# A decoder layer on one core: gate and projection products dealt out anew between the steps of two attention branches

## Chip, cores and metric

The kernel runs on one core of a Trainium2 chip. The metric is device time in microseconds (us) of one execution; lower is better. All tensors are fp32. The large products run in a split form: an fp32 matrix is taken apart into a rounded high part and the rest, and a product of two such pairs is made of three matmuls.

## The reference, cut to what matters

```python
h = rms_norm(x, g_mix)                       # x: 512 tokens x 1024
z = h @ w_in                                 # -> qa, ka, va, qb, kb, vb, gate logits gl
ya = swa_sink_attention(rms(qa), rms(ka), va, sinks, bias_a)   # window 128, 8 q heads, 2 kv heads
# differential branch, per head (4) and block of 128 queries:
p = softmax(where(causal, q @ k.T / 8 + bias_b, -inf))         # two maps, c = 0, 1
ob = (p[0] - lam * p[1]) @ vb
yb = rms_norm(ob, subln_b) * (1 - lam_init)
g = sigmoid(gl)                              # two gates of 1024
x = x + (g[0] * (ya @ w_br_a) + g[1] * (yb @ w_br_b)) @ w_o
u = causal_dwconv3(rms_norm(x, g_ffn) @ w_up)
x = x + (silu(u_gate) * u_value) @ w_down
```

## The kernel before, in words

All weights lie in one array of units of 128 x 1024. `wunit(u)` (L132) loads a unit over SP's queue, rounds it on ACT (L123, tile whi) and subtracts on POOL or DVE (L124, tile wlo); each call also starts the unit behind it in the fixed order `worder` (AHEAD = 1). So a unit's split is issued when the unit ahead of it begins, which is eight steps earlier for most units. `mm3` (L143) makes one **step** of three matmuls: L145 and L147 need whi, and one of L146 and L147 needs wlo.

The program has three stretches. First the query, key and value products of the window branch. Then, from about 52 to 305 us, both attention branches. Last the output product, the MLP and the down product, which are matmuls without a break.

In the middle stretch each unit of attention is a chain: PE scores, DVE adds the bias and takes the maximum, ACT takes the exponentials, DVE normalises, PE transposes, ACT and DVE round the transposed weights, PE multiplies with the values. PE would wait for each of these, so independent products are dealt between its steps: gates, the two differential projections DA and DB, the differential values VB and the window branch's output product. They stand in one queue, a `Stream`, in a fixed order. `fill(name, i)` takes so many steps from the queue's head as the table FILL says, and `until(name)` takes all that are left of one kind. PE, and PE alone, runs in the order in which the code is written (`manual_schedule`); the orders of DVE, ACT and POOL are made by the scheduler at build time, and each engine keeps its own order when it runs.

The window branch has eight units (four query blocks times two kv heads), here called window unit 0 to 7. Its queue holds three gates (24 steps), DA (32) and five gates (40): 96 steps. The loop is

```python
    for i in range(nu + 2):
        if i < nu:
            swa_score(*swa[i])
        fill("s1", i)
        if 0 <= i - 1 < nu:
            swa_trans(*swa[i - 1])
        fill("s2", i)
        if 0 <= i - 2:
            swa_av(*swa[i - 2])
        fill("s3", i)
```

Ahead of it stand `fill("q")`, the query transposes, `fill("k")`, the key transposes (L415) and `fill("k2")`. Behind it stand `fill("p0")`, `diff_parts` for head 0 (transposes L415, rounding in L424, L426, L436, L438, L439), `fill("p1")`, the same for head 1, and `until("ga")`, which takes what is left of the 96. Then the eight sigmoids of the first gates are issued (L486, on ACT), VB, the output product, DB and eight gates are put into the queue (160 steps), and `fill("p2")` follows.

The differential branch has sixteen units, four heads times four blocks, here differential unit 0 to 15. For unit i the code scores it (L443, L444; a[i] steps behind), then transposes unit i - 1 (L705; b[i - 1] steps behind). The product with the values of a head (L725, `diff_av`) comes once a head, heads 2 and 3 get their `diff_parts` ahead of units 8 and 9 (f steps behind), and DB is finished ahead of unit 6. Lines that the text names: L572 bias and maximum, L588 normalise, L597 transpose, L601 rest of the rounding, L614 and L616 the product with the values (window); L678, L683, L689, L705, L712, L725 the same steps (differential).

Of the kernel before, what the change touches and what calls it, by code (L numbers as in the profile page):

```python
# [59 lines left out]

FILL = dict(v=[9, 17, 25, 33], m=[0, 0, 0, 0], r=[4, 9, 13, 18], o=[7, 11, 15, 17], e=[1, 1, 0, 40], kv=4,
            up=3, warm=8, q=3, k=19, k2=4, s1=[0, 3, 2, 2, 2, 3, 3, 0, 0, 3],
            s2=[3, 1, 0, 3, 1, 3, 5, 2, 0, 1], s3=[3, 0, 4, 1, 3, 2, 1, 6, 0, 1], p0=4, p1=7, p2=6, ud=6,
            pd=[8, 9], f=[7, 0], a=[7, 1, 4, 6, 12, 3, 0, 3, 0, 1, 7, 2, 4, 0, 0, 7],
            b=[6, 2, 4, 4, 2, 7, 2, 1, 2, 0, 2, 2, 1, 0, 3, 2], c=[6, 0, 0, 2], d=[1, 1, 0, 5])
AHEAD = 1
EARLY = 5

# [2 lines left out]
def tile_decoder_layer(ctx: ExitStack, tc: tile.TileContext, x4, wall, cst_d, relb_d, oneh_d, xn_d, out):  # L73
# [35 lines left out]
    def at():  # L109
        return psum.tile([P, S], F32, tag="ps", name=nm("at"))  # L110
# [72 lines left out]
    def along_free(col, alloc, between=None):  # L183

        ch = stat.tile([P, NT], F32R, tag="colh", name=nm("colh"))
        cl = stat.tile([P, NT], F32, tag="coll", name=nm("coll"))
        nc.vector.tensor_copy(ch, col)
        nc.vector.tensor_tensor(cl, col, ch.bitcast(F32), ALU.subtract)
        ps = at()
        for i, part in enumerate((ch.bitcast(F32), cl)):  # L190
            dg = alloc().bitcast(F32R)
            for t in range(NT):
                nc.vector.tensor_scalar(dg[:, t * P:(t + 1) * P], ident, part[:, t:t + 1], None, ALU.mult)
            nc.tensor.matmul(ps, ones, dg, start=i == 0, stop=i == 1)
            if between is not None and i == 0:
                between()
        return ps
# [18 lines left out]
    ps = at()  # L216
    for i in range(FILL["warm"]):
        nc.tensor.matmul(ps, zero[:, :P], zero, start=True, stop=True)
# [269 lines left out]
    class Stream:  # L488
# [18 lines left out]
        def fill(self, n):  # L507
            while n > 0 and self.step():
                n -= 1
# [7 lines left out]
    def fill(name, i=None):  # L517
        fs.fill(FILL[name] if i is None else FILL[name][i])

# [123 lines left out]
    def diff_parts(z, hh):  # L643
        qs = q_parts(pair_T(z, hh * 256), gqa[:, 1:2])
        kh, kl = k_parts(pair_T(z, hh * 256 + P), cst[:, C_KNB:C_KNB + 1])
        return qs, kh, kl
# [90 lines left out]
    def diff_out(h):  # L737
        o, col = dpo.pop(h)
        r = along_free(col, otile, lambda: fs.fill(FILL["m"][h]))
        nc.vector.tensor_tensor(o, o, r, ALU.mult)  # L740
# [38 lines left out]
    def products(place):  # L779
        for h in range(4):  # L780
            if FILL["v"][h] == place:
                fs.until("vb")
# [4 lines left out]
    for i in range(len(todo) + 1):  # L787
        if i < len(todo):
            h, b = todo[i]
            if i == FILL["ud"]:  # L790
                fs.until("db")
            for h1 in (2, 3):
                if i == FILL["pd"][h1 - 2]:
                    qkt[h1] = diff_parts(zt[2], h1 - 2)
# [265 lines left out]
```

## Time and profile before

| | |
|---|---|
| median of 3 runs | 734.42 us (734.22 to 736.84) |
| profiled execution | 734.53 us |
| its span on the core | 732.7 us |
| mean granted TensorE clock | 0.988 |
| PE, DVE, ACT, POOL busy | 97%, 63%, 43%, 23% of the span |

The profiled execution is one run of the program with the hardware profiler; its own time is the span plus what lies around it (1.8 us). The three runs are timed without it.

### The profile page before, as it was taken

What the parts mean: (1) busy time and instruction counts of PE and PEld (TensorE: products, weight loads), DVE (VectorE), ACT (ScalarE), POOL (GpSimd) and SP (SyncE); (2) the same over time, 40 slices, a digit from 0 to 9 for tenths busy, and PEclk for the clock granted to TensorE, in tenths of its full rate; (3) what the DMA queues carried; (4) which work ended last, traced back from release to release, by engine and by line L of the source; (5) the groups of instructions that cost most, each with busy time, mean ns of one, the idle gap of its engine ahead of it and who ended that gap; (6) DMA issues with size and microseconds to landing.
All of it is one profiled execution on the core that took longest, in us unless ns stands there. A gap on an engine that the chain in (4) does not pass through costs nothing.

```text
span 732.7 us, 8962 instructions
## 1 busy us (share of the span) xinstructions
PE 708.0 (97%) x3312; PEld 585.0 (80%) x3312; DVE 458.3 (63%) x940; ACT 315.3 (43%) x522; POOL 167.5 (23%) x130
## 2 busy tenths in 40 slices
PE   8999996999999889989999999999999999999998
PEld 5887785878887768868888888888888888888888
DVE  5688799576409798595438876766666674322220
ACT  6554674754336436444325444444444442221220
POOL 1154235454435320083400201110110110000000
PEclk9999998999999999999999999999999999999999
DMA  8762111132132020225421332322322322333310
GB/s 310 278 219 87 58 58 46 42 114 82 63 105 69 30 81 35 86 78 167 155 89 59 115 114 87 104 97 87 109 92 88 115 80 85 132 114 102 114 65 30
DMA packets 21820, 74.04 MB, mean 101 GB/s; under 512 B 2612, under 2 KB 3152, under 8 KB 21648
## 3 DMA queue, kind: packets, MB, share of 16 engines
q1 hardware_dynamic: 18976, 65.02, 26.2%
q0 software_dynamic: 1360, 6.34, 2.7%
q10 hardware_dynamic: 1440, 2.11, 0.8%
q8 instruction: 26, 0.43, 0.2%
q14 instruction: 18, 0.15, 0.1%
HBM read 71.34 MB, written 4.47 MB: 103 GB/s over the span
## 4 chain that ended last, share of the span: by engine, by line
PE 83%; DVE 12%; ACT 3%; issue 1%; DMA 1%; SPq 0%; ACTq 0%; DVEq 0%
PE pj L145 26%; PE pj L146 25%; PE pj L147 25%; ACT s L581 1%; PE at L725 1%; DVE s L588 1%; DVE g L850 1%; DVE qv L439 1%; DVE s L572 1%; DVE qv L438 1%; DVE g L849 1%; DMA g<-in_x_dram 1%; PE at L415 1%; PE at L705 1%; PE pj L321 1%
## 5 line engine op out<-in xcount | busy, mean ns | idle before, releaser
L123 ACT ACTIVATE whi<-raw 128x1024 fp32r<-128x1024 f32 (+1 forms) x117 | 121.7, 1044 | 178.3 <-PE pj L146 121.1
L145 PE MATMUL pj<-xg,whi 128*128 128x512 f32 x480 | 190.6, 397 | 0.0
L147 PE MATMUL pj<-xg,wlo 128*128 128x512 f32 x480 | 188.1, 392 | 0.0
L146 PE MATMUL pj<-xg,whi 128*128 128x512 f32 x480 | 187.9, 392 | 0.0
L124 DVE TENSOR_TENSOR wlo<-raw,whi 128x1024 fp32r<-128x1024 f32 (+1 forms) x84 | 103.4, 1234 | 81.9 <-ACT whi L123 81.8
L147 PEld LDWEIGHTS pj<-xg,wlo 128*128 128x128 f32 x480 | 90.7, 189 | 19.1
L145 PEld LDWEIGHTS pj<-xg,whi 128*128 128x128 f32 x480 | 90.8, 189 | 17.9
L146 PEld LDWEIGHTS pj<-xg,whi 128*128 128x128 f32 x480 | 90.8, 189 | 17.7
L124 POOL TENSOR_TENSOR wlo<-raw,whi 128x1024 fp32r<-128x1024 f32 x33 | 79.6, 2417 | 107.6 <-ACT whi L123 88.3
L916 DVE TENSOR_TENSOR u<-pj,rbc 128x512 f32<-128x512 f32 x44 | 30.2, 690 | 48.3 <-PE pj L147 48.3
L145 PE MATMUL pj<-whi,xg 128*128 128x512 f32 (+1 forms) x156 | 58.3, 373 | 0.0
L146 PE MATMUL pj<-wlo,xg 128*128 128x512 f32 (+1 forms) x156 | 57.6, 369 | 0.1
L147 PE MATMUL pj<-whi,xg 128*128 128x512 f32 (+1 forms) x156 | 57.4, 368 | 0.0
L919 ACT ACTIVATE yc<-u,cst 128x512 f32<-128x512 f32 x44 | 35.4, 810 | 4.5 <-DVE u L916 4.5
L145 PE MATMUL pj<-y,whi 128*128 128x512 f32 (+1 forms) x95 | 37.1, 391 | 0.0
L147 PE MATMUL pj<-y,wlo 128*128 128x512 f32 (+1 forms) x95 | 36.4, 383 | 0.2 <-POOL wlo L124 0.2
L147 PE MATMUL pj<-qv,wlo 128*128 128x512 f32 (+1 forms) x94 | 35.4, 377 | 1.1 <-DVE wlo L124 1.1
L146 PE MATMUL pj<-y,whi 128*128 128x512 f32 (+1 forms) x95 | 36.2, 381 | 0.0
L921 DVE SCALAR_TENSOR_TENSOR yc<-u,cst,yc 128x510 f32<-128x510 f32 x44 | 34.8, 794 | 1.3
L145 PE MATMUL pj<-qv,whi 128*128 128x512 f32 (+1 forms) x94 | 35.4, 376 | 0.0
L920 DVE SCALAR_TENSOR_TENSOR yc<-u,cst,yc 128x511 f32<-128x511 f32 x44 | 33.7, 768 | 0.0
L146 PE MATMUL pj<-qv,whi 128*128 128x512 f32 (+1 forms) x85 | 32.3, 380 | 1.5 <-POOL qv L853 1.5
(213 smaller groups left out, 1159.2 us busy)
## 6 DMA issues: line engine op xcount, KB each, us to landing
raw<-in_w_dram SPq DMA_DIRECT2D x109, 512.0 KB, 3.3
raw<-in_w_dram SPq DMA_DIRECT2D x8, 384.0 KB, 3.2
scr<-scr POOLq DMA_DIRECT2D x1, 2304.0 KB, 11.7
xnat<-in_xn_dram SPq DMA_DIRECT2D x2, 1024.0 KB, 9.4
tmp<-in_x_dram POOLq DMA_DIRECT2D x8, 256.0 KB, 3.2
g<-in_x_dram SPq DMA_DIRECT2D x7, 256.0 KB, 7.0
out_dram<-x ACTq DMA_DIRECT2D x7, 256.0 KB, 2.0
bias_a<-scr POOLq DMA_DIRECT2D x1, 1024.0 KB, 7.3
```

Source lines behind the costliest of these rows:

```text
L123: nc.scalar.activation(hi[:, :width], raw[:, :width], AF.Copy)
L124: eng.tensor_tensor(lo[:, :width], raw[:, :width], hi[:, :width].bitcast(F32), ALU.subtract)
L145: nc.tensor.matmul(ps, a[0], b[0], start=start, stop=False)
L146: nc.tensor.matmul(ps, a[0], b[1], start=False, stop=False)
L147: nc.tensor.matmul(ps, a[1], b[0], start=False, stop=stop)
L321: nc.tensor.matmul(banks[t][:, :width], xg[k][a][:, t * P:(t + 1) * P], wk[b], start=(a, b) == (0, 0), stop=False)
L415: nc.tensor.transpose(ps[:, t * P:(t + 1) * P], zs[t][:, c0:c0 + P], ident)
L438: nc.vector.tensor_copy(k[o, :], k[s, :].bitcast(F32))
L916: nc.vector.tensor_tensor(u, ps, rbc2, ALU.mult)
L919: nc.scalar.activation(y, u, AF.Identity, bias=cst[:, C_CB + ch:C_CB + ch + 1], scale=cw[2])
L920: nc.vector.scalar_tensor_tensor(y[:, 1:S], u[:, 0:S - 1], cw[1], y[:, 1:S], ALU.mult, ALU.add)
L921: nc.vector.scalar_tensor_tensor(y[:, 2:S], u[:, 0:S - 2], cw[0], y[:, 2:S], ALU.mult, ALU.add)
```

## The change

Only the table FILL changes. No product is added or removed, and each queue keeps its order; what changes is how many steps of the queue lie at each place.

```diff
-            up=3, warm=8, q=3, k=19, k2=4, s1=[0, 3, 2, 2, 2, 3, 3, 0, 0, 3],
-            s2=[3, 1, 0, 3, 1, 3, 5, 2, 0, 1], s3=[3, 0, 4, 1, 3, 2, 1, 6, 0, 1], p0=4, p1=7, p2=6, ud=6,
-            pd=[8, 9], f=[7, 0], a=[7, 1, 4, 6, 12, 3, 0, 3, 0, 1, 7, 2, 4, 0, 0, 7],
-            b=[6, 2, 4, 4, 2, 7, 2, 1, 2, 0, 2, 2, 1, 0, 3, 2], c=[6, 0, 0, 2], d=[1, 1, 0, 5])
+            warm=8, q=7, k=19, k2=4, s1=[0, 3, 2, 2, 2, 3, 3, 0, 0, 3], s2=[4, 3, 0, 3, 1, 7, 5, 2, 0, 1],
+            s3=[3, 0, 1, 5, 6, 2, 2, 6, 0, 1], p0=4, p1=5, p2=8, ud=6, pd=[8, 9], f=[9, 0],
+            a=[5, 1, 8, 7, 10, 2, 0, 3, 0, 1, 7, 4, 6, 0, 0, 5],
+            b=[6, 2, 4, 4, 2, 7, 2, 1, 2, 0, 2, 0, 1, 1, 2, 2], c=[7, 0, 0, 1], d=[1, 0, 0, 5])
```

Summed up, the window queue stands at 71 of its 96 steps when window unit 7 has been scored before, and at 87 now. It is empty one step behind the loop's last s1, so that p0, p1 and `until("ga")` find nothing, though the table still names 4 and 5.

First place, ACT between the two branches. Before, the sigmoids (L486) stand on both sides of the rounding of head 0 and head 1 (L424, L436); these are the last of them:

```order
L486 ACTIVATE g_1534<-g_1534 128x512
L424 ACTIVATE qv_1569<-at_1564,gqa 64x512
L424 ACTIVATE qv_1570<-at_1564,gqa 64x512
L436 ACTIVATE qv_1582<-at_1575,cst 64x512
L436 ACTIVATE qv_1583<-at_1575,cst 64x512
L486 ACTIVATE g_1595<-g_1595 128x512
L123 ACTIVATE whi_1611<-raw_1609 128x1024
L123 ACTIVATE whi_1661<-raw_1659 128x1024
L683 ACT_TABLE_LOAD
```

The same place now; whi_1611 is in both programs the second unit of VB:

```order
L436 ACTIVATE qv_1588<-at_1580,cst 64x512
L486 ACT_TABLE_LOAD
L486 ACTIVATE g_666<-g_666 128x512
L486 ACTIVATE g_699<-g_699 128x512
L486 ACTIVATE g_732<-g_732 128x512
L486 ACTIVATE g_1189<-g_1189 128x512
L486 ACTIVATE g_1273<-g_1273 128x512
L486 ACTIVATE g_1366<-g_1366 128x512
L486 ACTIVATE g_1458<-g_1458 128x512
L486 ACTIVATE g_1526<-g_1526 128x512
L123 ACTIVATE whi_1611<-raw_1609 128x1024
L683 ACT_TABLE_LOAD
```

All eight sigmoids and the load of their table moved behind the rounding of both heads, and whi_1611 stands behind all of it.

Second place, DVE at window units 2 and 3. Before, unit 2 (sm_900, s_880) is summed and normalised ahead of the first maximum of unit 3 (s_952):

```order
L584 TENSOR_TENSOR sm_900<-sm_900,sk_898 128x4
L586 RECIPROCAL rc_907<-sm_900 128x4
L588 TENSOR_SCALAR s_880<-s_880,rc_907 128x256 x4
L619 TENSOR_TENSOR o_928<-at_929,o_928 64x512
L572 ISA s_952,mx_953<-at_954,bias_a 128x256
```

Now, where unit 2 is sm_927 and s_907, and unit 3 is s_964:

```order
L572 ISA s_964,mx_965<-at_966,bias_a 128x256
L572 ISA mx_965 128x1
L584 TENSOR_TENSOR sm_927<-sm_927,sk_925 128x4
L572 ISA s_964,mx_965<-at_966,bias_a 128x256
L572 ISA mx_965 128x1
L586 RECIPROCAL rc_934<-sm_927 128x4
L601 TENSOR_TENSOR ptl_952<-at_946,pth_951 128x512
L588 TENSOR_SCALAR s_907<-s_907,rc_934 128x256 x4
```

Two maxima of unit 3 moved ahead of the normalising of unit 2.

Third place, PE at the transpose of differential unit 11 (L705) and the product with the values of head 2 behind it (L725). Before, two steps lie between them:

```order
L705 MATMUL at_2763<-ident,p_2657 128x128 x4
L145 MATMUL pj_2704<-xg_178,whi_2632 128x512
L146 MATMUL pj_2704<-xg_179,whi_2632 128x512
L147 MATMUL pj_2704<-xg_178,wlo_2633 128x512
L145 MATMUL pj_2704<-xg_189,whi_2632 128x512
L146 MATMUL pj_2704<-xg_190,whi_2632 128x512
L147 MATMUL pj_2704<-xg_189,wlo_2633 128x512
L725 MATMUL at_2776<-ath_2540,vbh_1836 128x512
```

Now:

```order
L145 MATMUL pj_2777<-xg_146,whi_2694 128x512
L146 MATMUL pj_2777<-xg_147,whi_2694 128x512
L147 MATMUL pj_2777<-xg_146,wlo_2695 128x512
L705 MATMUL at_2787<-ident,p_2660 128x128 x4
L725 MATMUL at_2794<-ath_2555,vbh_1830 128x512
```

Both steps moved ahead of the transpose.

## Rows read from the trace of the kernel before

**Rows 1.** The page's part 1: busy time, share of the span, instructions.
```profile
PE 708.0 (97%) x3312; PEld 585.0 (80%) x3312; DVE 458.3 (63%) x940; ACT 315.3 (43%) x522; POOL 167.5 (23%) x130
```

**Rows 2.** PE's waits: who for whom, us in total, times, longest.
```profile
PE at L597 <- DVE s L588: 7.5, 5, 4.5
PE at L705 <- DVE p L689: 3.7, 3, 2.1
```

**Rows 3.** Timelines, window unit 6: start, us, instruction, [idle before it, releaser].
```profile
108.48 0.42 DVE L572 CUSTOM_DVE_ANT_0 s<-at,bias_a 128x256 f32<-128x256 f32 x1
...
118.06 0.48 PE L597 MATMUL at<-ident,s 128*128 128x128 f32 x1 [4.47 <-DVE s L588]
```

**Rows 4.** Stretches: PE, PEld, DVE, ACT, POOL busy, granted TensorE clock, DMA.
```profile
70.00:75.00 5.00, 3.26 (x18) 2.50 (x17) 4.46 (x16) 1.42 (x5) 2.35 (x1) 1.00 0.06 11
116.59:123.41 6.82, 4.21 (x13) 3.15 (x14) 6.75 (x17) 1.97 (x3) 3.36 (x4) 0.50 0.00 1
242.89:246.28 3.39, 3.39 (x12) 2.88 (x11) 2.38 (x11) 1.36 (x5) 0.00 (x0) 0.50 0.02 5
266.78:270.18 3.40, 3.40 (x11) 2.54 (x10) 3.33 (x12) 2.65 (x6) 0.11 (x1) 0.50 0.02 5
```

**Rows 5.** Timeline of PE, 146 to 147 us: first matmul of two steps in succession.
```profile
146.31 0.39 PE L145 MATMUL pj<-whi,xg 128*128 128x512 f32 x1
...
146.99 0.39 PE L145 MATMUL pj<-whi,xg 128*128 128x512 f32 x1
```

**Rows 6.** Timeline of ACT, 134 to 150 us.
```profile
134.51 0.59 ACT L618 ACTIVATE o<-at 64x512 f32<-64x512 f32 x1 [1.91 <-PE at L616]
135.86 0.63 ACT L623 ACTIVATE y<-o 128x512 fp32r<-128x512 f32 x1 [0.76 <-DVE o L619]
136.51 1.28 ACT L486 ACT_TABLE_LOAD   x1
...
138.86 1.37 ACT L424 ACTIVATE qv<-at,gqa 64x512 fp32r<-64x512 f32 x2
140.26 1.39 ACT L436 ACTIVATE qv<-at,cst 64x512 fp32r<-64x512 f32 x2
141.67 2.71 ACT L486 ACTIVATE g<-g 128x512 f32<-128x512 f32 x5
...
147.76 1.99 ACT L123 ACTIVATE whi<-raw 128x1024 fp32r<-128x1024 f32 x2
```

**Rows 7.** Timeline of POOL from 148 us.
```profile
148.94 7.12 POOL L124 TENSOR_TENSOR wlo<-raw,whi 128x1024 fp32r<-128x1024 f32 x3 [8.77 <-issue]
```

**Rows 8.** Timeline of PE from head 1's transposes to the second unit of VB.
```profile
143.37 1.03 PE L415 MATMUL at<-ident,z 128*128 128x128 f32 x8
...
150.85 0.39 PE L145 MATMUL pj<-whi,xg 128*128 128x512 f32 x1
151.39 0.50 PE L146 MATMUL pj<-wlo,xg 128*128 128x512 f32 x1
```

**Rows 9.** Timeline of PE in the differential branch: its longer waits.
```profile
240.33 0.33 PE L443 MATMUL at<-qv,qv 128*128 128x128 f32 x1 [1.71 <-DVE qv L438]
...
265.47 0.52 PE L705 MATMUL at<-ident,p 128*128 128x128 f32 x3 [2.11 <-DVE p L689]
```

**Rows 10.** Differential unit 15: DVE's normalising, and PE's transpose of it.
```profile
290.49 0.75 DVE L689 SCALAR_TENSOR_TENSOR p<-p,drc 128x512 f32<-128x512 f32 x1
...
292.08 0.60 PE L705 MATMUL at<-ident,p 128*128 128x128 f32 x4
```

**Rows 11.** Timelines of DVE and POOL: window units 0 and 3, and a split.
```profile
70.82 3.01 DVE L588 TENSOR_SCALAR s<-s,rc 128x128 f32<-128x128 f32 x4
71.40 2.35 POOL L124 TENSOR_TENSOR wlo<-raw,whi 128x1024 fp32r<-128x1024 f32 x1 [5.62 <-ACT whi L123]
...
84.50 0.41 DVE L572 CUSTOM_DVE_ANT_0 s<-at,bias_a 128x256 f32<-128x256 f32 x1
...
89.12 1.14 DVE L588 TENSOR_SCALAR s<-s,rc 128x256 f32<-128x256 f32 x4
```

More of the change, by code (lines that the diff above doesn't have):

```diff
@@ L59 @@
 U_N = U_DN + 8 * 3
-FILL = dict(v=[9, 17, 25, 33], m=[0, 0, 0, 0], r=[4, 9, 13, 18], o=[7, 11, 15, 17], e=[1, 1, 0, 40], kv=4,
-            up=3, warm=8, q=3, k=19, k2=4, s1=[0, 3, 2, 2, 2, 3, 3, 0, 0, 3],
-            s2=[3, 1, 0, 3, 1, 3, 5, 2, 0, 1], s3=[3, 0, 4, 1, 3, 2, 1, 6, 0, 1], p0=4, p1=7, p2=6, ud=6,
-            pd=[8, 9], f=[7, 0], a=[7, 1, 4, 6, 12, 3, 0, 3, 0, 1, 7, 2, 4, 0, 0, 7],
-            b=[6, 2, 4, 4, 2, 7, 2, 1, 2, 0, 2, 2, 1, 0, 3, 2], c=[6, 0, 0, 2], d=[1, 1, 0, 5])
+FILL = dict(v=[9, 17, 25, 33], m=[0, 0, 0, 0], r=[4, 9, 13, 18], o=[7, 11, 15, 17], e=[1, 1, 0, 40], kv=4, up=3,
+            warm=8, q=7, k=19, k2=4, s1=[0, 3, 2, 2, 2, 3, 3, 0, 0, 3], s2=[4, 3, 0, 3, 1, 7, 5, 2, 0, 1],
+            s3=[3, 0, 1, 5, 6, 2, 2, 6, 0, 1], p0=4, p1=5, p2=8, ud=6, pd=[8, 9], f=[9, 0],
+            a=[5, 1, 8, 7, 10, 2, 0, 3, 0, 1, 7, 4, 6, 0, 0, 5],
+            b=[6, 2, 4, 4, 2, 7, 2, 1, 2, 0, 2, 0, 1, 1, 2, 2], c=[7, 0, 0, 1], d=[1, 0, 0, 5])
 AHEAD = 1
```

## The prediction, before the change was run

> **What bounds the kernel now.** I read the busy shares first: PE is busy 97% of the span [rows 1], so a step that is only moved costs or gives nothing by itself. What can change is time in which PE stands still, and time in which it runs at the lower of its two clocks. PE's waits come next. The normalising of the window branch (L588) holds up the transposes (L597) for 7.5 us in five waits, that of the differential branch (L689) the transposes L705 for 3.7 in three [rows 2]. The timelines show where. Window unit 6 has its first maximum at 108.48 and its first transpose at 118.06, after 4.47 us of idle [rows 3]: the norm of the DA products lies between in DVE's order. The table by stretches gives the price behind such idle time. From 116.59 to 123.41 the granted clock was 0.50 (1.2 of 2.4 GHz) and PE worked 4.21 us in it, and it was 0.50 again for 3.39 us from 242.89 and 3.40 us from 266.78 [rows 4], each time behind a wait of 1.7 us or more [rows 9]. Work at half clock takes twice as long, so these three cost 2.1, 1.7 and 1.7 us. An idle time of 1.74 us between 70 and 75 us, on the other hand, left the clock at 1.00 [rows 4]. The profiled run took 734.53 us, 0.1 over the median of the three; the sum is made against it. About 0.5%, or 3.7 us, is what a measurement of this kernel can tell from no change.
>
> A step costs 0.68 us [rows 5].
>
> **Window branch, what goes.** The norm of the DA products follows when step 57 of the queue is asked for. Before, that is behind the score of unit 5, and the norm reaches into unit 6, whose chain on DVE takes 9.6 us to the first transpose [rows 3]; without a norm, unit 3 took from its first maximum at 84.50 to the end of its normalising at 90.26, 5.8 us [rows 11]. Now step 57 comes behind the score of unit 4. Unit 4 has twelve steps, a score, a transpose and a product with values between its own score and transpose (8.2 and some 2.7, together 10.9 us), unit 5 twelve steps and unit 6 seven (4.8 and 2.7). So each chain fits under the work in front of its transpose, the norm under that of unit 4. Unit 0 has one step more. I take the whole 7.5 out, and the 2.1 of low clock: **-9.6**.
>
> **Window branch, what stays.** Unit 2 gets 3 steps between score and transpose instead of 6, and on DVE two maxima of unit 3 now stand ahead of its normalising, as the second excerpt shows; the score of unit 3 is only two steps ahead of that transpose. Two maxima, a rounding and the normalising (1.14 us for four, [rows 11]) lie behind that score, against two steps of cover: I take 1.1. The last product with values has one step in front of it where four stood; I take 0.5, and 0.3 for the rest. **+1.9**, between 0.8 and 4.5 (the upper end: unit 2 waits a collision of 1.9 longer, see below, and unit 0 keeps half of its 1.74).
>
> **Between the branches.** This is the term that decides. The queue of 96 is empty, so both heads' transposes follow each other, then come the 8 steps of p2 (the first unit of VB), the score of differential unit 0, and the second VB unit, whose rounding whi_1611 ACT does only behind all eight sigmoids. Count from the end E of the last window product. ACT: the eviction and the wait for the first transposes 0.8, then L424 twice for two heads (1.40 a pair), L436 likewise (1.41), L623 0.65, table load 1.30, eight sigmoids at 2.73 / 5 = 0.55, whi 1.0: 13.8. All these are rows of the present run, taken from start to start where the next row stands there [rows 6]. POOL then takes 7.12 / 3 = 2.4 [rows 7], so wlo is there at E + 16.3. PE: before, from the transposes of head 1 at 143.37 to the first matmul on this unit at 150.85 it took 7.5 us for eight transposes, nine steps and a score [rows 8]; now there are eight more transposes (1.0 at most) and one step less: E + 7.8. One matmul fits into the hole when whi has come. PE loses 16.3 - 7.8 - 0.2 = 8.3 us. Before, POOL was just in time: the second matmul came 0.54 behind the first instead of 0.23 [rows 8]. An idle time of 8 us brings the clock down as the one of 4.47 did; I take the same 2.1, with bounds 1.0 and 3.4 (the latter two stretches of 3.4 at half clock). **+10.4**, between 8.5 and 12.4. Behind it differential unit 0 is ready: its exponentials follow whi_1611 by a table load, some 17 us after E, and PE has six steps and a score to do from E + 16. So the wait ahead of the first L705 goes: of the 3.7 us in three waits [rows 2] 2.1 belong to unit 10 [rows 9], and I give unit 0 a third of the rest, 0.5. With the 0.2 or so of POOL: **-0.7**.
>
> **Units 1 to 7.** Only steps among units that did not wait; DB is finished at the same place ahead of unit 6. Nothing.
>
> **Unit 8.** f has two more steps ahead of the score that waits 1.71 us for the rounding of the keys [rows 9]. That takes off 1.36, leaves 0.35, and I expect the clock to stay up: **-3.1**, or -1.4 if it falls all the same.
>
> **Unit 10.** Two more steps ahead of the transpose that waits 2.11 us [rows 9], one less (d) earlier. If DVE is the limit from head 3's rounding on, only one step's worth, 0.68, is won; if the score sets the time, 1.36. I take the first, and the clock's 1.7: **-2.4**, between -3.8 (the whole wait) and -0.7.
>
> **Units 11 and 15.** Both steps behind the transpose of unit 11 are gone (third excerpt), and ACT's rounding (L712) must be waited for: at most the two steps, 1.4; ACT also has more time to get ahead, so that I take less than half. **+0.6**, 0 to 1.4. Three steps less lie between score and transpose of unit 15; its normalising ended at 291.24 and the transpose began at 292.08, a slack of 0.84 against 2.0 [rows 10]. **+0.9**, 0 to 2.
>
> Sum: -9.6 + 1.9 + 10.4 - 0.7 - 3.1 - 2.4 + 0.6 + 0.9 = -2.0, so 732.5 us.
>
> **A rule of the skill.** Normalising window unit 0 took 3.01 us for four instructions while POOL split a weight from 71.40 on, against 1.14 for unit 3, with twice the columns, when POOL was still [rows 11]: a collision of 1.9. The Trainium skill (Advanced Engine Details and Errata, VectorE Performance Modes) says that Vector's second port is shared with GpSimd, so that the two block each other; the trace agrees. By that rule a split could fall on the normalising of window unit 2 or of differential unit 10, since both move against POOL. The sum would then be 1.9 higher, 734.4.
>
> **Rivals.** *Faster.* The second half gives more: the transpose of unit 10 stops waiting altogether (-3.8), units 11 and 15 cost 0.3 together, and the low clock behind the sigmoids costs 1.0: 728.7. For it speaks that DVE stood still for 1.0 of the 3.39 us from 242.89, just ahead of head 3's rounding; against it, that it was busy for 3.33 of the 3.40 from 266.78 [rows 4]. It decides at unit 10: a wait under 0.5 there. *Faster for another reason:* PE does not lose the 8.3 at whi_1611. Then it would wait at the first transpose until E + 17 instead, some 5 us, and the time would be 729. The order on ACT speaks against it. *Slower.* The hole of window unit 6 is not filled but moves: DA's norm on window unit 4 outlasts the 10.9 us of cover. Its price is at most that of the old hole, 5.6 us (the 7.5 less unit 0's 1.74 and a small one) and 2.1 of clock: 740.2. For it speaks that the old chain with the norm took 9.6 to the first transpose and was longer to the last [rows 3]; against it, the 10.9. It decides when the chain takes over 11. *No effect:* the clock falls at units 8 and 10 all the same, +3.4, 735.9; or the splits collide, 734.4; or gains and losses cancel.
>
> **Chances.** The forecast with its neighbours of no visible effect 0.52, faster 0.35 (0.30 for the second half, 0.05 for no loss at whi_1611), slower 0.13. The forecast's own range is 730.8 to 736. The range takes in both faster cases and the lower part of the slower one: 727.5 to 738.
>
> **What would show it.** No wait of L597 on L588 over 2 us around 110 to 125 us; PE idle some 8 us, ended by POOL's wlo, right behind the first score of the differential branch at about 145 us; the clock at 0.50 only there and no more at 243 and 267 us; the L443 of unit 8 waiting under 0.5 us. If PE does not stand still at the sigmoids, or stands still at window unit 4, the prediction is wrong.

## The result, and the profile after

| | before | now |
|---|---|---|
| median | 735.08 us of 5 runs (734.22 to 736.84) | 730.59 us of 5 runs (730.34 to 732.34) |
| ratio of the times | | 0.9938, 95% interval 0.9918 to 0.9959 |
| second series, other runs | 735.42 us of 17 runs | 731.51 us of 6 runs; 0.9940 (0.9924 to 0.9956) |
| profiled execution, span | 734.53, 732.7 us | 730.34, 728.6 us |

The change makes the kernel 0.6% faster. The forecast was 732.5 us with a range of 727.5 to 738, and "no visible effect" as the likeliest case; the time lies in the range, 0.2 us below the forecast's own part of it (730.8 to 736), and the change of 4.5 us by the medians is a little over the 3.7 that the prediction took as visible.

Part 1 of the page now, which answers to [rows 1]: PE's busy time fell by 2.1 us at the same number of instructions. In the four stretches at 0.50 before, from 7.36 us to 270 us, PE worked 14.4 us; in the two now it works 7.0.

```profile
PE 705.9 (97%) x3312; PEld 582.6 (80%) x3312; DVE 450.0 (62%) x940; ACT 316.0 (43%) x522; POOL 167.0 (23%) x130
```

PE's waits of the changed kernel (us in total, times, longest), which answer to [rows 2]:

```profile
PE pj L145 <- ACT whi L123: 5.9, 1, 5.9
PE pj L146 <- POOL wlo L124: 1.7, 1, 1.7
PE at L597 <- DVE s L588: 1.5, 1, 1.5
...
PE at L705 <- DVE p L689: 1.3, 2, 1.0
...
PE at L444 <- DVE qv L439: 1.0, 2, 0.5
PE at L194 <- DVE o L193: 0.7, 1, 0.7
PE at L725 <- ACT ath L712: 0.7, 1, 0.7
```

The 7.5 us for the normalising of the window branch are down to one wait of 1.5, and two new ones stand at the head: 5.9 us for a rounded weight and 1.7 for its rest. PE's timeline has the places, first the transpose of window unit 2, then the second unit of VB, then the four waits at the score of differential unit 8 (which answer to [rows 9]) and the first wait behind the transpose of unit 10:

```profile
84.53 0.59 PE L597 MATMUL at<-ident,s 128*128 128x128 f32 x2 [1.54 <-DVE s L588]
...
146.74 0.79 PE L145 MATMUL pj<-whi,xg 128*128 128x512 f32 x1 [5.89 <-ACT whi L123]
149.22 0.79 PE L146 MATMUL pj<-wlo,xg 128*128 128x512 f32 x1 [1.69 <-POOL wlo L124]
...
238.82 0.33 PE L443 MATMUL at<-qv,qv 128*128 128x128 f32 x1 [0.43 <-DVE qv L438]
239.68 0.30 PE L444 MATMUL at<-qv,qv 128*128 128x128 f32 x1 [0.54 <-DVE qv L439]
240.14 0.30 PE L443 MATMUL at<-qv,qv 128*128 128x128 f32 x1 [0.16 <-DVE qv L438]
240.93 0.44 PE L444 MATMUL at<-qv,qv 128*128 128x128 f32 x1 [0.49 <-DVE qv L439]
...
265.19 0.50 PE L194 MATMUL at<-o,ones 128*128 128x512 f32 x1 [0.73 <-DVE o L193]
```

Why the weight is late is read from ACT's timeline, the counterpart of [rows 6]:

```profile
140.18 1.28 ACT L486 ACT_TABLE_LOAD   x1
141.48 4.26 ACT L486 ACTIVATE g<-g 128x512 f32<-128x512 f32 x8
145.65 1.04 ACT L123 ACTIVATE whi<-raw 128x1024 fp32r<-128x1024 f32 x1
146.71 1.28 ACT L683 ACT_TABLE_LOAD   x1
148.00 0.40 ACT L683 ACTIVATE p<-p,dnmx 128x128 f32<-128x128 f32 x1
```

The rounding of the weight has nothing to do with the sigmoids; it stands behind a table load and eight of them in ACT's order, and begins when they are done. The stretches, in the columns of [rows 4], show what the clock did behind the waits:

```profile
145.25:152.08 6.83, 3.65 (x8) 2.57 (x9) 0.96 (x4) 5.49 (x9) 4.52 (x2) 0.50 0.23 77
240.83:244.24 3.41, 3.31 (x11) 2.93 (x12) 2.58 (x9) 1.96 (x6) 0.00 (x0) 0.50 0.11 46
266.00:270.00 4.00, 4.00 (x21) 3.38 (x20) 3.62 (x12) 1.65 (x7) 0.00 (x0) 1.00 0.28 111
```

It is at 0.50 (1.2 of 2.4 GHz) between the branches for 3.65 us of work, which cost 1.8, and at unit 8 for 3.31, which cost 1.7; at 1.00 behind unit 10, where it was 0.50 before.

Where the 4.19 us between the two profiled executions lie is found by setting the same PE instruction of both against each other. The start gives 1.04 us before the first place that the change touches: before, the clock was 0.50 from 7.36 to 10.77 us, now it is 1.00 there. The start differs from one execution to the next in the runs below too (the kernel with the same table, profiled again, lost 0.5 of it), so it is none of the change. The window branch and the stretch between the branches give 0.5 together, unit 8 gives 1.3, units 10 and 11 2.65, and the tail (units 13 to 15) takes 1.3 back.

### The profile page after: what moved, and what is told of

The parts are those of the page before. It is cut to its first block, busy times and chain, and to the rows that moved or that the text cites. A ratio compares the mean times of both kernels' runs of the same rounds, so it can differ in the third digit from the quotient of the medians.

```text
span 728.6 us, 8960 instructions
## 1 busy us (share of the span) xinstructions
PE 705.9 (97%) x3312; PEld 582.6 (80%) x3312; DVE 450.0 (62%) x940; ACT 316.0 (43%) x522; POOL 167.0 (23%) x130
## 3 DMA queue, kind: packets, MB, share of 16 engines
q10 hardware_dynamic: 1440, 2.11, 0.8%
## 4 chain that ended last, share of the span: by engine, by line
PE 78%; DVE 8%; issue 2%; ACT 2%; POOL 0%; DVEq 0%; ACTq 0%; POOLq 0%
PE pj L145 24%; PE pj L147 24%; PE pj L146 24%; PE at L725 1%; DVE g L850 1%; PE at L597 1%; PE at L444 1%; DVE g L849 1%; DVE o L193 1%; PE at L443 1%; DVE p L678 1%; DVE p L689 1%; PE at L705 1%; PE at L614 0%; DVE wlo L124 0%
## 5 line engine op out<-in xcount | busy, mean ns | idle before, releaser
L145 PE MATMUL pj<-whi,xg 128*128 128x512 f32 (+1 forms) x156 | 59.5, 382 | 6.0 <-ACT whi L123 5.9
L147 PE MATMUL pj<-whi,xg 128*128 128x512 f32 (+1 forms) x156 | 58.1, 372 | 0.1
L145 PEld LDWEIGHTS pj<-whi,xg 128*128 128x128 f32 x156 | 29.8, 191 | 11.3 <-ACT whi L123 6.0
L146 PEld LDWEIGHTS pj<-wlo,xg 128*128 128x128 f32 x156 | 29.9, 191 | 7.0 <-POOL wlo L124 2.2
L145 PE MATMUL pj<-qv,whi 128*128 128x512 f32 (+1 forms) x94 | 35.4, 376 | 0.0
```

The costliest lines, as they stand in the source:

```text
L145: nc.tensor.matmul(ps, a[0], b[0], start=start, stop=False)
L146: nc.tensor.matmul(ps, a[0], b[1], start=False, stop=False)
L147: nc.tensor.matmul(ps, a[1], b[0], start=False, stop=stop)
```

## Experiments

**1 and 2. The change in two halves.** First the window half alone (with p2 and a[0], which belong together, since 6 + 7 = 8 + 5), then the differential half alone.

```diff
 (window half, on the kernel before)
-q=3, ... s2=[3, 1, 0, 3, 1, 3, 5, 2, 0, 1], s3=[3, 0, 4, 1, 3, 2, 1, 6, 0, 1], p0=4, p1=7, p2=6, a=[7, ...
+q=7, ... s2=[4, 3, 0, 3, 1, 7, 5, 2, 0, 1], s3=[3, 0, 1, 5, 6, 2, 2, 6, 0, 1], p0=4, p1=5, p2=8, a=[5, ...
 (differential half, on the kernel before)
-f=[7, 0], a=[7, 1, 4, 6, 12, 3, 0, 3, 0, 1, 7, 2, 4, 0, 0, 7],
-b=[6, 2, 4, 4, 2, 7, 2, 1, 2, 0, 2, 2, 1, 0, 3, 2], c=[6, 0, 0, 2], d=[1, 1, 0, 5]
+f=[9, 0], a=[7, 1, 8, 7, 10, 2, 0, 3, 0, 1, 7, 4, 6, 0, 0, 5],
+b=[6, 2, 4, 4, 2, 7, 2, 1, 2, 0, 2, 0, 1, 1, 2, 2], c=[7, 0, 0, 1], d=[1, 0, 0, 5]
```

> The kernel before with the window half of the change alone (q, s2, s3, p0, p1, p2 and a[0]). By the reading of the two traces (theory): the 9.5 us of waits and low clock in the window branch go, 7.6 us of waiting and 1.8 us of low clock appear at the second VB unit, and the differential branch is as before, so the time is 0.5 us under the kernel before, within 1.5 us of it either way, which this measurement can't tell from no change. Rival: the sigmoids' stall is hidden or cheaper than it looks in one profile, and the window half carries most of the gain: 3 us or more under the kernel before.

> The kernel before with the differential half alone (f, a[2] on, b, c, d). Theory: unit 8 gives 1.3 us (the clock falls there all the same), units 10 and 11 together 2.6, the tail takes 1.3 back, so 2.7 us under the kernel before, between 1.5 and 4, with no wait of PE at the sigmoids. Rival (the prediction's step, that the clock stays up at unit 8 when the first wait there is under 0.5 us): 4.4 under, with a granted clock of 1.00 at about 243 us.

Measured: window half 734.17 us against 735.20, ratio 0.9982 (0.9969 to 0.9995); differential half 732.70, ratio 0.9960 (0.9945 to 0.9976). The two products make 0.9942, the whole change 0.9938: the halves add up. So the window half, for which most entries of the table were changed, is worth 0.2%, with an interval that reaches to 0.05%; set against the profile before, and without the start, its profile gives 0.2 us. It has both sides of the exchange: one wait for L588 where five stood, and the two waits of the result, at the same size in PE's timeline:

```profile
146.97 0.79 PE L145 MATMUL pj<-whi,xg 128*128 128x512 f32 x1 [5.90 <-ACT whi L123]
149.46 0.80 PE L146 MATMUL pj<-wlo,xg 128*128 128x512 f32 x1 [1.69 <-POOL wlo L124]
```

In the differential half the clock was 0.50 behind unit 8 again (241.86 to 245.27), which speaks against the rival of experiment 2.

**3. The split ahead of the sigmoids.** Is the stall the place in ACT's order?

```diff
+    v = worder[wnext[0]]
+    units[v] = split_unit(v, 1024, nc.gpsimd)
+    wnext[0] += 1
     sig = ExitStack()
     with tc.issue_after(swa_acts[-1].ins), tc.issue_after(swa_acts[-2].ins):
         for i in sigmoids(0):
```

> The changed kernel with the split of the second VB unit issued ahead of the eight sigmoids instead of behind them. Theory: the wait of 7.6 us at this unit goes, but the exponentials of differential unit 0 still stand behind the sigmoids and one rounding, so that PE waits at the first transpose of the branch instead, for 4 to 6 us, and the low clock stays: 2 to 4 us under the changed kernel. Rival: the 7.6 us and the 1.8 of low clock go as a whole: 9.4 under the changed kernel. Second rival: nothing is won, since the sigmoids hold up the same amount wherever PE meets them: within 1 us.

Measured: 725.54 us, ratio to the kernel before 0.9876 (0.9855 to 0.9897), so 5 us under the changed kernel (4.6 by the ratios): more than the theory's 2 to 4 and less than the first rival's 9.4. The mechanism is the theory's. The waits of 5.89 and 1.69 are gone, and PE waits at the first transpose of the branch, since the exponentials stand behind the sigmoids too. ACT's timeline, and PE's:

```profile
143.58 4.28 ACT L486 ACTIVATE g<-g 128x512 f32<-128x512 f32 x8
147.87 1.28 ACT L683 ACT_TABLE_LOAD   x1
...
151.19 0.48 PE L705 MATMUL at<-ident,p 128*128 128x128 f32 x1 [3.61 <-DVE p L689]
```

**4. The same edit on the kernel before**, as a control.

> The kernel before with the same edit as the run that split the second VB unit ahead of the sigmoids, as a control. Theory: the 5 us that the edit won in the changed kernel came from the sigmoids that the change had put ahead of this split. Before, the split is just in time, so the edit can win only the 0.5 and 0.15 us that PE waits there and at the first differential transpose: within 1.5 us of the kernel before. Rival: the edit is good in itself, whatever the order of the sigmoids: 3 us or more under the kernel before.

Measured: 734.30 us against 735.68, ratio 0.9982 (0.9971 to 0.9993), within the theory's 1.5. The edit is worth 5 us only behind the change. So the change did open this wait, and the sigmoids ahead of the split are its cause.

**5. Six more steps there.** On the kernel of experiment 3:

```diff
-a=[5, 1, 8, 7, 10, ...
+a=[11, 1, 8, 7, 4, ...
```

> The changed kernel with the early split and six steps more behind the score of differential unit 0 (a[0] = 11), taken from behind unit 4 (a[4] = 4), whose transposes come 18 us after their normalising. Theory: what is left of the stall is the wait of 3.6 us at the first transpose of the branch with the 1.7 us of low clock behind it; six steps are 4.1 us, so both go and nothing takes their place: 720 us, between 719 and 722, some 5 under the kernel with the early split alone. Rival: the low clock comes from something else there (the score's short products), and only the wait goes: 722. Second rival: the wait moves to the next weight unit or to the transposes of unit 4: no gain over the kernel with the early split.

Measured: 727.07 us, ratio 0.9883 (0.9868 to 0.9898): no gain over experiment 3. The theory fell, the second rival holds. The wait at the transpose is gone, and PE now comes to the third unit of VB, whose split stands behind the sigmoids as the second's did. PE's timeline:

```profile
150.07 0.50 PE L145 MATMUL pj<-whi,xg 128*128 128x512 f32 x1 [2.58 <-ACT whi L123]
...
152.56 0.65 PE L146 MATMUL pj<-wlo,xg 128*128 128x512 f32 x1 [1.98 <-POOL wlo L124]
```

That is 4.56 us where 3.61 stood. More steps need more rounded weights, and all of ACT's work for PE stands in one line.

**6. The sigmoids elsewhere**: behind the exponentials of differential unit 2. The two loads of ACT's tables go there with them; the profiles of both kernels have five loads in all.

```diff
-    with tc.issue_after(swa_acts[-1].ins), tc.issue_after(swa_acts[-2].ins):
-        for i in sigmoids(0):
-            sig.enter_context(tc.issue_after(i.ins))
...
             diff_score(h, b)
+            if i == 2:
+                with tc.issue_after(exps[-1].ins), tc.issue_after(exps[-2].ins):
+                    for g in sigmoids(0):
+                        sig.enter_context(tc.issue_after(g.ins))
```

> The changed kernel with the eight sigmoids issued behind the exponentials of differential unit 2 instead of ahead of those of unit 0. If the stall is the sigmoids' place in ACT's order, the 7.6 us at the second VB unit and the 1.8 of low clock go. What comes in their place: at the new place the next weight unit's rounding stands behind sigmoids and two table loads, some 6 to 7 us of ACT, and PE has about ten steps there. If the ten steps cover it: 8 to 9.4 under the changed kernel. If not, PE waits 2 to 5 us at that unit: 4 to 7 under. Rival: the stall moves as a whole, within 1.5 us of the changed kernel.

Measured: 729.23 us, ratio 0.9909 (0.9887 to 0.9931), 1.4 us under the changed kernel by the medians and 2.1 by the ratios: the rival, or just outside its bound of 1.5. The 7.6 us are gone, but 0.46 and 1.31 us at the first scores, 1.50 at the first transpose and 1.70 at a weight's rest have come, and the low clock is still there (148.19 to 155.02). PE's timeline has the two longest:

```profile
149.25 0.48 PE L705 MATMUL at<-ident,p 128*128 128x128 f32 x1 [1.50 <-DVE p L689]
...
168.87 0.50 PE L147 MATMUL pj<-y,wlo 128*128 128x512 f32 x1 [1.70 <-POOL wlo L124]
```

**7. And steps to cover that**, on the kernel of experiment 6:

```diff
-p2=8, a=[5, 1, 8, ...
+p2=11, a=[9, 1, 2, ...
```

> The changed kernel with the sigmoids behind the exponentials of differential unit 2, as in the earlier run with that edit, and with steps dealt to what PE waited for in that run: p2 = 11 for 8, a[0] = 9 for 5, a[2] = 2 for 8. Theory: of the waits left there (0.46 and 1.31 us at the first scores, 1.50 at the first transpose, 1.70 at a late weight half) seven steps cover the first three, and the low clock behind them goes too: 4.5 us under that run, about 725, and at least level with the kernel that splits the unit ahead of the sigmoids. Rival: DVE is the limit there (in that run ACT waited 5.6 us for the maximum of unit 0), and the steps only move the wait: within 1.5 us of that run.

Measured: 728.27 us, ratio 0.9890 (0.9874 to 0.9907), 1 us under experiment 6 (1.4 by the ratios). The theory was right at the first scores and the first transpose, where no wait is left, and wrong on the whole: PE now comes earlier to the unit whose split stands behind the sigmoids at their new place, and the 1.70 has become 4.80, as PE's timeline shows:

```profile
168.69 0.50 PE L145 MATMUL pj<-y,whi 128*128 128x512 f32 x1 [2.60 <-ACT whi L123]
...
171.62 0.79 PE L147 MATMUL pj<-y,wlo 128*128 128x512 f32 x1 [2.20 <-POOL wlo L124]
```

**8. Both**: on experiment 7, the split of that unit issued ahead of the sigmoids, by the three lines of experiment 3 put into the `if i == 2`.

> The last run with the sigmoids behind unit 2's exponentials and the steps dealt anew, with one edit more: the split of the weight unit that PE waited for there (2.60 us for whi, 2.20 for wlo) is issued ahead of the sigmoids. Theory: what is late is always the weight half that stands behind the sigmoids in ACT's order, wherever they are; with eight steps more in hand PE does not reach the unit behind it before ACT and POOL are through, so the 4.8 us go and the low clock behind them: 728.3 less 4.8 and 1.5 to 3, about 721, the fastest of all. Rival: it goes as with six more steps at the first place, where the wait moved to the next unit at the same size: within 1.5 us of 728.3.

Measured: 722.68 us against 735.56, ratio 0.9832 (0.9816 to 0.9847): 5.6 us under experiment 7, some 8 under the changed kernel, and the fastest of all; the theory said about 721. What it would be without the added steps of experiment 7 was not run. The stretch from 150 to 180 us, in the columns of [rows 4], has PE busy throughout at the full clock:

```profile
150.00:180.00 30.00, 30.00 (x145) 24.97 (x144) 21.73 (x61) 21.00 (x42) 12.06 (x5) 1.00 0.23 72
```

**9. Unit 8 without its waits.**

```diff
-f=[9, 0], b=[6, 2, 4, 4, 2, 7, 2, 1, 2, ...
+f=[12, 0], b=[6, 2, 4, 4, 2, 7, 2, 0, 0, ...
```

> The changed kernel with f[0] = 12 instead of 9, that is three steps (2.04 us) more between the transposes of head 2 and the score of differential unit 8, taken from behind units 7 and 8. Theory: the four waits at this score, 1.62 us together, are one lateness of DVE and go as a whole, and with them the stretch at 0.50: 3.3 us under the changed kernel, 727.3. Rival: the clock falls at about 241 us without any wait (it did so with 2.90 and with 1.62): 1.6 under. Second rival: units 8 and 9 lose what unit 8 wins: no change.

Measured: 732.74 us, ratio 0.9959 (0.9945 to 0.9973): nothing won over the changed kernel, by the ratios even 1.5 us lost (in the profiled execution the start alone took 2.4 us more, with a low clock at 11 us). At unit 8 the theory holds: one wait of 0.17 us is left at its score, the clock stays at 1.00, and set against the changed kernel PE gains 2.7 us there. All of it is lost at the transpose of unit 10, which waits 2.62 us. The timelines of POOL, DVE and PE of this kernel show why:

```profile
261.88 2.34 POOL L124 TENSOR_TENSOR wlo<-raw,whi 128x1024 fp32r<-128x1024 f32 x1 [4.27 <-ACT whi L123]
...
262.09 2.54 DVE L689 SCALAR_TENSOR_TENSOR p<-p,drc 128x384 f32<-128x384 f32 x1
...
264.78 0.30 PE L705 MATMUL at<-ident,p 128*128 128x128 f32 x1 [2.62 <-DVE p L689]
```

The same split and the same instruction in the changed kernel's timelines of POOL and DVE:

```profile
255.55 2.39 POOL L124 TENSOR_TENSOR wlo<-raw,whi 128x1024 fp32r<-128x1024 f32 x1 [6.44 <-ACT whi L123]
255.99 1.97 DVE L159 TENSOR_TENSOR t<-t,tv 128x4 f32<-128x4 f32 x1
...
260.71 0.61 DVE L689 SCALAR_TENSOR_TENSOR p<-p,drc 128x384 f32<-128x384 f32 x1
...
262.13 2.40 POOL L124 TENSOR_TENSOR wlo<-raw,whi 128x1024 fp32r<-128x1024 f32 x1 [4.19 <-ACT whi L123]
```

The normalising of unit 10 took 0.61 us when the weight split came behind it and 2.54 when it began 0.2 us into the split: 1.93 more, the size that [rows 11] showed at window unit 0. The prediction drew from the Trainium skill (Advanced Engine Details and Errata, VectorE Performance Modes) that Vector and GpSimd block each other at a shared port; the trace agrees, at one of the two places that the prediction named, though in another kernel. That section speaks of Vector instructions that use two ports; whether L689 is one of them no run shows, and none took the split away to isolate it.

**10. f alone**: `f=[7, 0]` to `f=[9, 0]` on the kernel before.

> The kernel before with f[0] = 9 instead of 7 and nothing else, to see whether the terms of units 8 and 10 add up. Theory: unit 8's first wait falls from 1.71 to 0.4 and unit 10's stays at 2.1 us with its low clock behind it: 1.3 under the kernel before. Rival: the steps are taken from what covers unit 10, whose wait grows by about 1.3: no change.

Measured: 734.92 us against 735.42, ratio 0.9983 (0.9972 to 0.9994), 0.5 to 1.3 us by medians and ratio. The time is near the theory's, but its reason fell: unit 10's wait did not stay. In this profile it went from 2.11 to 0.11 us, with the clock at 1.00 from 266 to 270 us, though unit 10's own entries were those of before. PE's timeline has no bracket there any more:

```profile
263.97 0.33 PE L705 MATMUL at<-ident,p 128*128 128x128 f32 x1
```

The timelines of POOL and DVE show what went. First the kernel before, where DVE works without a break from the roundings of head 3 (L426, 249.90) to the end of unit 10's normalising (265.32), and a split falls into that time:

```profile
253.79 2.40 POOL L124 TENSOR_TENSOR wlo<-raw,whi 128x1024 fp32r<-128x1024 f32 x1 [4.97 <-ACT whi L123]
254.29 1.92 DVE L687 TENSOR_TENSOR drc<-drc,neglam 128x1 f32<-128x1 f32 x1
```

Then the kernel with f alone. A split comes earlier there and meets another instruction (L689, 2.40 us from 247.22), where DVE had stood idle for 2.66 us before; L687 is alone:

```profile
247.06 2.41 POOL L124 TENSOR_TENSOR wlo<-raw,whi 128x1024 fp32r<-128x1024 f32 x1
...
255.17 0.15 DVE L687 TENSOR_TENSOR drc<-drc,neglam 128x1 f32<-128x1 f32 x1
```

From L426 to the end of that normalising DVE takes 15.4 us before and 13.1 now: 1.8 less for L687, 0.6 less for an eviction of a gate (L472) that no longer stands there. PE had waited 2.11. In the changed kernel it is 13.0, by the same two (split at 245.42, L687 0.15 us). So the two steps moved a split, and by the trace its collision was most of that wait; no run isolates it.

Later rows of the same timeline have the bill: 0.78 us at the transpose of unit 14 and 1.10 and 0.22 behind it, where the kernel before had no wait.

```profile
288.52 0.52 PE L705 MATMUL at<-ident,p 128*128 128x128 f32 x3 [0.78 <-DVE drc L687]
291.51 0.47 PE L194 MATMUL at<-o,ones 128*128 128x512 f32 x1 [1.10 <-DVE o L193]
292.20 0.50 PE L194 MATMUL at<-o,ones 128*128 128x512 f32 x1 [0.22 <-DVE o L193]
```

**11. Window unit 2**, the one long wait left in the window branch.

```diff
-s1=[0, 3, 2, 2, ...  s3=[3, 0, 1, 5, ...
+s1=[0, 3, 2, 5, ...  s3=[3, 0, 1, 2, ...
```

> The changed kernel with three steps moved from behind the products of window unit 1 to behind the score of unit 3, so that they lie ahead of the transpose of unit 2 and still ahead of unit 3's. Theory: the wait of 1.54 us there goes and nothing else moves: 1.5 under the changed kernel (the clock was 1.00 behind this wait in the changed kernel's profile and 0.50 in that of the kernel with the early split, so up to 3.2 where it fell). Rival: DVE's new order there holds up another unit: no gain, or a loss of up to 2.

Measured: 734.29 us, ratio 0.9979 (0.9966 to 0.9993), so about 3 us over the changed kernel; the rival, and more. The wait at unit 2 went, and the score of window unit 4 waited as long, because DVE's order had changed and the rests of the roundings stood behind unit 3's normalising. DVE's timeline, and PE's:

```profile
90.19 1.14 DVE L588 TENSOR_SCALAR s<-s,rc 128x256 f32<-128x256 f32 x4
91.25 1.28 DVE L601 TENSOR_TENSOR ptl<-at,pth 128x512 fp32r<-128x512 f32 x2
...
91.98 0.39 PE L443 MATMUL at<-qv,qv 128*128 128x256 f32 x1 [1.56 <-DVE ptl L601]
```

Up to the transpose of unit 4 this is level with the changed kernel. The loss comes behind it: 0.49 us of waiting at unit 5's transposes (one of the four normalisings ahead of them took 2.47 us beside a split that began at 113.06), small pieces up to the last window product (2.2 us by then), and a longer low clock between the branches (145.14 to 155.38, 4.75 us of work in it instead of 3.65).

**12. The changed kernel again**, unedited.

> The changed kernel once more, nothing edited, for a second profile of the same program. Theory: the waits are those of the program and come out the same within 0.1 us each, but whether the clock falls behind a wait of 1 to 2 us (window unit 2, differential unit 8) differs from one execution to the next, as it differed between runs of kernels that have the same waits at these places; the time is 730.6 within 1.5. Rival: the clock's falls belong to the program as the waits do: 0.50 behind unit 8 and 1.00 behind window unit 2 as in the first profile.

Measured: 731.51 us, ratio 0.9940 (0.9924 to 0.9956). From 60 us on every wait is the same within 0.02 us, and so are the clock's falls: 0.50 from 241.49 to 244.90, 1.00 behind window unit 2. For this program the rival holds; across programs see the last section.

## Why the prediction was right, and where it was not

**Window waits, -9.6: right.** No transpose waits at units 0, 1 and 3 to 7, and the low clock at 117 us is gone. DA's norm under unit 4 fits; the slower rival did not come. The prediction counted the steps of units 2, 5 and 6 too low by those directly behind their own score: the table gives 5, 15 and 10 for its 3, 12 and 7, so the cover was larger still. At unit 0 one step, 0.68 us, is not what took the 1.74 away, and its normalising still meets a split (3.05 us, 3.01 before). DVE came to its first maximum 1.3 us behind the score instead of 4.6, since the rounding L438 ahead of it took 0.42 us now and 2.40 before, beside another split, and an eviction no longer stood there.

**Window stays, +1.9: 1.5.** Unit 2 waits 1.54 us where 1.1 was taken. The order of the second excerpt is there, one maximum and a rounding (1 us) between the sum and the normalising, but a collision stands ahead of it: unit 1's normalising met a split that it had not met before. The timelines of DVE and POOL in the changed kernel, then DVE's before:

```profile
75.52 3.06 DVE L588 TENSOR_SCALAR s<-s,rc 128x128 f32<-128x128 f32 x4
76.11 2.39 POOL L124 TENSOR_TENSOR wlo<-raw,whi 128x1024 fp32r<-128x1024 f32 x1 [3.94 <-ACT whi L123]
...
77.09 0.87 DVE L588 TENSOR_SCALAR s<-s,rc 128x128 f32<-128x128 f32 x4
```

By the trace these 2.2 us more held up the maxima of unit 2, which was scored at 75.83 and had its first maximum at 79.10; no run isolates them. So the collision that the prediction feared at unit 2 came one unit earlier. The 0.5 at the last product and the 0.3 for the rest did not appear, and a wait of 0.45 at 63.7 us, which the sum had not listed, is gone too.

**Between the branches, +10.4: 9.4.** 5.89 and 1.69 us of waiting for the expected 8.3, and 1.8 of low clock for 2.1. ACT, POOL and PE came as they were counted; POOL ended at E + 16.1 (149.17, with E = 133.07) against 16.3. Experiments 3 and 4 show that the cause is the sigmoids ahead of the split. The -0.7 behind it is right: neither the first transpose nor POOL's 0.15 waits.

These terms together were +2.0 in the forecast and are -0.5 between the two profiles: 0.4 from the window, 1.0 from the sigmoids, 0.45 from the unlisted wait, and some 0.6 in pieces too small to name. The runs agree on the sign: the window half is 0.2% faster, 1 to 1.3 us.

**Unit 8, -3.1: it was -1.3.** This is the step that failed. The first wait fell to 0.43 (0.35 forecast), but "I expect the clock to stay up" did not hold: the other three waits, 1.19 us, were left out of the thought. (They stood there before too and did not change; what the first wait ends on, the CAST of L438, took 1.62 us beside a split before and 1.66 now, against 0.42 for the same CAST of head 3.) The bound of -1.4, for the case that the clock falls all the same, was the value.

**Unit 10, -2.4, and unit 11, +0.6: -2.65 together instead of -1.8.** The whole wait of 2.11 went, and 0.73 us behind it came; the clock stayed up. The reason was wrong: experiment 10 shows that the two steps at unit 8 alone remove this wait, without the steps that the prediction paid it with, and the timelines there show why: a collision on DVE and an eviction went, 2.4 us. By its sign at unit 10, a wait under 0.5, the faster rival held; its other conditions did not, since units 11 to 15 cost 1.6 and not 0.3, and the low clock behind the sigmoids 1.8 and not 1.0. Unit 11's wait grew from 0.36 to 0.69 us, 0.3 for the 0.6 taken.

**Unit 15, +0.9: 1.3**, spread over units 13 to 15.

So the sum of -2.0 missed by 2.2 in the profiled pair, of which 1.0 is the start; what is left, some 1.2, is the balance of -2.5 in the first half, -0.9 at units 10 and 11, and +1.8 and +0.4 at unit 8 and the tail. The runs put the change at -4.4 us with an interval of some 1.5 either way, at the edge of what these terms explain. That the sum came so near is in part luck, since the terms missed to both sides. That 7.5 us of waits and 2.1 of low clock were traded for 7.6 and 1.8 is why a change to some twenty entries moved the time by 0.6%.

## What to carry to other kernels

When independent work is moved to fill one hole, ask what is left for the next one, and read it from the order of the engine that prepares the work: here the sigmoids, needed by nobody soon, stood ahead of a weight that PE needed at once, and the filled hole came back at its full size. Adding steps only moves PE on to the next piece that stands behind the same block (experiments 5 and 7); the block has to go where there is slack, the piece behind it has to be prepared ahead of it, and only both together, with the steps dealt anew, gave 1.7%. A table that moves work on one engine also moves it against the others, so a wait that a step should cover can come back through a reordered queue (experiment 11) or a collision (experiment 9), and a wait that goes can owe it to a collision that moved away (experiment 10).

## What the hardware showed that was not expected

**The clock behind a short wait.** The same four waits at unit 8 (0.39 to 0.43, 0.54, 0.16 and 0.49 us) were followed by a granted clock of 0.50 in six profiles (both of the change, experiments 2, 3, 6 and 11) and by 1.00 in four (experiments 5, 7, 8 and 10). In experiment 5 the stretches read, with the waits in the first:

```profile
236.00:240.00 4.00, 2.39 (x13) 1.59 (x12) 3.87 (x9) 0.19 (x1) 0.56 (x1) 1.00 0.39 131
240.00:244.00 4.00, 4.00 (x28) 3.44 (x27) 2.56 (x9) 3.53 (x9) 1.72 (x2) 1.00 0.01 2
```

The wait of 1.5 us at window unit 2 left it at 1.00 in eight profiles and brought it to 0.50 in one (experiment 3, 85.80 to 89.21 us), and in experiment 9 even 2.62 us at unit 10 left it up, as the 2.11 us there did in experiment 4. A term of 1.7 us for the clock behind one or two us of waiting is thus a chance and not a price; behind the waits of 5.6 us (at 117) and 7.6 (at 147) it fell in every profile that had them.

**A tiny instruction can take the whole collision.** DVE's L159 on four numbers a partition took 1.97 us beside POOL's split and 0.16 without; it ended at 257.96, the split at 257.94. PE did not wait at the next transpose, that of unit 10. In the kernel before, two such instructions stood ahead of that transpose (L687 with 1.92 us and L160 with 2.26, beside the splits from 253.79 and 258.40), and PE waited 2.11 us. So it matters how many of the splits fall into a stretch in which DVE has no slack.
